# Gate products on the two 64-row halves of the array, and a tile of its own for the backward scan

## The chip, the cores and the metric

The kernel runs on one core of one Trainium2 chip. The metric is the device time of one execution in microseconds; the median of three runs before the change is 1204.66 (1204.58 to 1204.77). The engines are called by the profile's names: PE is TensorE (matmuls), PEld its weight loads, ACT is ScalarE, DVE is VectorE, POOL is GpSimd, SP is SyncE, which issues most DMAs.

## What is computed

Two layers over 512 tokens of 1024 channels, in float32. Each layer projects the normalised input to queries, keys, values, a recurrent input and a gate branch, runs neighbourhood attention (8 heads) beside a two-way gated recurrence (512 channels), normalises both, projects them back, and then runs a gated MLP with a width-3 convolution. The part that the change touches is the recurrence:

```python
def rg_lru(x, w_gate, b_gate, lam, reverse):
    bsz, s, _ = x.shape
    xb = x.reshape(bsz, s, N_LRU_BLOCKS, LRU_BLOCK)
    g = jnp.einsum("bsnc,gncd->gbsnd", xb, w_gate).reshape(2, bsz, s, D_LRU)
    g = g.astype(jnp.float32) + b_gate.astype(jnp.float32)[:, None, None, :]
    r_gate = jax.nn.sigmoid(g[0])
    i_gate = jax.nn.sigmoid(g[1])
    log_a = -LRU_C * r_gate * jax.nn.softplus(-lam.astype(jnp.float32))
    a = jnp.exp(log_a)
    u = jnp.sqrt(-jnp.expm1(2.0 * log_a)) * (i_gate * x.astype(jnp.float32))
    return linear_scan(a, u, reverse).astype(x.dtype)
...
        xc = depthwise_conv(x_rec, conv_lru_w[l], conv_lru_b[l], LRU_PAD)
        rec_f = rg_lru(xc, lru_w[l, 0], lru_b[l, 0], lru_lam[l, 0], reverse=False)
        rec_b = rg_lru(xc, lru_w[l, 1], lru_b[l, 1], lru_lam[l, 1], reverse=True)
        rec = (rec_f + rec_b) * jax.nn.gelu(gate, approximate=True)
```

The gate weights are block-diagonal: each of the 8 blocks of 64 channels has a 64x64 matrix per direction (forward, backward) and gate (r, i).

## The kernel before

Activations lie with channels in the 128 partitions and the 512 tokens in the free dimension, so an activation tile is 128x512. Every float32 operand of a large product is split into a rounded part and a rest (`hi`, `lo`, or names ending in `h`, `l`), and `mm3` (L243 to L245) makes a product of three matmuls: hi x hi, lo x hi, hi x lo. Weights come in chunks of up to 128x1024 by DMA (`raw`), are rounded on ACT (L205, `hi`) and subtracted on DVE (L206, `lo`), three chunks ahead of use. In layer 1 the gate, query, key and other input weights are not split in place: they were split during the MLP of layer 0 (`split_later`, L222 and L223), written to memory (`kept`), and are loaded in two halves as they are needed.

The mixing part of a layer follows a list of steps, `MIX`, which sets the order in the program text; a scheduler then orders each engine's instructions by it, with some marked urgent. `V` steps are value products, `c` the convolution of a block of 128 recurrent channels (`xc`, split into `xcs`), `t` the gates of such a block, `q`, `k` and `g` the query, key and gate-branch products (`a` and `b` are their halves of 12 matmuls), `S` the scores of a head, `T` the transposes of its probabilities (`ptw`, `pte`), `P` its product with the values (`o`), `u` copies of value edges on POOL, `e` the end of the gate branch (gelu, product with `fb`), `o` the output projection. PSUM banks come from small pools: three (`ps_mm`) for q, k, g and gate products, two for scores, two for transposes, one for `o`. A product can therefore wait for the bank that an earlier product's reader has not yet read.

`lru_gates` handles one block t of 128 channels, that is two of the 64-channel blocks. For each direction d and gate g it makes one full 128x128 product from a weight block that has the two 64x64 matrices on its diagonal and zeros elsewhere: 4 products of 3 matmuls (`gp`). ACT takes a tanh of each (L564: `w` for r, `ti` for i), then for each direction an exponential (`a`, L567), a tanh (L568), a square (L570), and one square root over both directions (L576, tile `w2` of 128x1024, of which there is one). DVE multiplies (L571, L572, L578), scans forward into `fb` (L581) and backward into `w` (L584), and adds the two (L586).

ACT's functions lie in tables, and a change of table is an instruction of its own (ACT_TABLE_LOAD). At the end of the kernel the scaled output is written in pieces of 4, 3 and 1 blocks (L485, L486).

Of the kernel before, what the change touches and what calls it, by code (L numbers as in the profile page):

```python
# [108 lines left out]
def encoder(ctx: ExitStack, tc: tile.TileContext, x_d, w_d, cols_d, bias_d, out_d):  # L109
# [102 lines left out]
    def split_later():  # L212
# [4 lines left out]
        for h in range(width(i) // 512):  # L217
            raw = p_t.tile([P, 512], F32, tag="t", name=f"lraw{i}{h}")
            nc.gpsimd.dma_start(raw, w_d[i][:, 512 * h:512 * h + 512])
            hi = p_fb.tile([P, 512], F32R, tag="fb", name=f"lhi{i}{h}")  # L220
            lo = p_fb.tile([P, 512], F32R, tag="fb", name=f"llo{i}{h}")
# [286 lines left out]
    def layer(l, xn):  # L508
# [24 lines left out]
        def convolve(t):  # L533
# [13 lines left out]
        pair = {}  # L547
# [2 lines left out]
        def lru_gates(t, ds):  # L550
            if 0 in ds:
                pair["c"] = chunk("gate", l, (t, 0))
            if 0 in ds:
                pair["w"], pair["work"] = p_w2.tile([P, 2 * T], F32, tag="w2", name=f"w2{l}{t}"), []
            c, both, work = pair["c"], pair["w"], pair["work"]
            for d in ds:
                w = both[:, d * T:(d + 1) * T]
                ti = big(p_t, "t", f"ti{l}{t}{d}")
# [6 lines left out]
                i = (l * 2 + d) * 4 + t  # L565
                a = big(p_t, "t", f"a{l}{t}{d}")
                nc.scalar.activation(a, w, AF.Exp, scale=spn[:, i:i + 1], bias=spn[:, i:i + 1])  # L567
# [421 lines left out]
```

## Time and profile before

| | |
|---|---|
| median of three runs | 1204.66 us (1204.58 to 1204.77) |
| the profiled execution, its span | 1204.35 us, 1202.6 us |
| mean granted clock | 0.996 |
| busy: PE, PEld | 1188.4 us (99%), 992.1 us (83%) |
| busy: DVE, ACT, POOL | 752.9 us (63%), 511.7 us (43%), 114.0 us (9%) |
| chain that ended last | PE 91%, ACT 4%, DVE 3% |
| where the gates lie | about 45 to 165 us (layer 0), 640 to 760 us (layer 1) |

The profiled execution is 1.75 us longer than its span. "Busy" is the sum of instruction durations; matmul records overlap, so the step from one start to the next tells what a matmul costs. Only a wait on PE, or more work on it, moves the end of this kernel directly; the idle time of the other engines matters where PE comes to need their result.

### The profile page before, as it was taken

Reading aid. Unit: us, or ns where it says so; the run is one execution under the profiler, and the core shown is the slowest. Engines: PE = TensorE matmul, PEld = TensorE weight load, DVE = VectorE, ACT = ScalarE, POOL = GpSimd, SP = SyncE. Lnnn points to the kernel's source line nnn. Section 1 sums busy time; section 2 is a strip of 40 time slices with the busy share of each in tenths; the row PEclk is TensorE's granted clock in tenths of the full one; section 3 lists DMA queues with packets and bytes.
Section 4 is the critical chain, followed back from the end, with each engine's and each line's share of the span. In section 5 each row is a group of like instructions: output and inputs, shape, how many; then the busy total and the mean of one; then the engine's idle time right before and its main releaser. Section 6 shows DMA issues by size and latency. Waiting matters only on the chain.

```text
span 1202.6 us, 14575 instructions
## 1 busy us (share of the span) xinstructions
PE 1188.4 (99%) x5534; PEld 992.1 (83%) x5534; DVE 752.9 (63%) x1226; ACT 511.7 (43%) x753; POOL 114.0 (9%) x230
## 2 busy tenths in 40 slices
PE   9999999999999999999999999999999999999996
PEld 8878888888888888888888888888888888888886
DVE  7988967776644567653736679587555336565443
ACT  6668854434321334422408578354233213333231
POOL 1102110123210122200002012000000000000000
PEclk9999999999999999999999999999999999999998
DMA  7222214376643376733256442232323232323222
GB/s 237 82 87 89 82 38 139 106 237 236 221 164 103 134 231 215 237 115 104 88 176 200 130 159 71 62 112 90 98 96 104 90 105 88 104 89 105 88 70 70
DMA packets 51046, 151.86 MB, mean 126 GB/s; under 512 B 6432, under 2 KB 9632, under 8 KB 50976
## 3 DMA queue, kind: packets, MB, share of 16 engines
q1 hardware_dynamic: 41792, 122.21, 31.1%
q0 software_dynamic: 8640, 28.32, 7.2%
q8 instruction: 43, 0.70, 0.2%
q10 hardware_dynamic: 544, 0.40, 0.1%
q14 instruction: 27, 0.22, 0.1%
HBM read 129.93 MB, written 20.97 MB: 125 GB/s over the span
## 4 chain that ended last, share of the span: by engine, by line
PE 91%; ACT 4%; DVE 3%; issue 1%; DVEq 0%; POOLq 0%; POOL 0%; ACTq 0%
PE dn L243 7%; PE dn L245 7%; PE dn L244 7%; PE pl L243 7%; PE pa L243 7%; PE pa L244 7%; PE pl L244 7%; PE pa L245 7%; PE pl L245 7%; PE out L245 2%; PE out L243 2%; PE out L244 2%; PE s L690 1%; PE xr L243 1%; PE up L243 1%; PE xr L244 1%
## 5 line engine op out<-in xcount | busy, mean ns | idle before, releaser
L205 ACT ACTIVATE hi<-raw 128x1024 fp32r<-128x1024 f32 (+1 forms) x189 | 197.6, 1046 | 380.5 <-PE dn L244 154.3
L206 DVE TENSOR_TENSOR lo<-raw,hi 128x1024 fp32r<-128x1024 f32 (+1 forms) x189 | 227.8, 1206 | 134.7 <-ACT hi L205 133.3
L845 DVE TENSOR_TENSOR ua<-pa,g_ffn_rb 128x512 f32<-128x512 f32 x44 | 30.4, 692 | 104.5 <-PE pa L245 104.5
L853 ACT ACTIVATE uc<-uc,cols 128x512 f32<-128x512 f32 x48 | 34.8, 724 | 116.2 <-DVE uc L851 116.1
L854 DVE TENSOR_TENSOR ua<-pl,uc 128x512 f32<-128x512 f32 x44 | 30.3, 689 | 45.0 <-PE pl L245 43.4
L467 POOL TENSOR_TENSOR fin_r<-fin_ms,expo 128x2 f32<-128x2 f32 x2 | 1.4, 696 | 377.0 <-DVE fin_ms L465 377.0
L851 DVE SCALAR_TENSOR_TENSOR uc<-ua,cols,uc 128x511 f32<-128x511 f32 x48 | 36.0, 751 | 1.6
L228 POOL DMA_DIRECT2D kept<-lhi x36 | 19.5, 542 | 182.1 <-ACT lhi L222 180.2
L849 DVE SCALAR_TENSOR_TENSOR uc<-ua,cols,uc 128x511 f32<-128x511 f32 x48 | 35.8, 746 | 0.1
L705 ACT ACTIVATE prob<-prob,mx 128x192 f32<-128x192 f32 (+1 forms) x64 | 27.5, 431 | 16.1 <-DVE mx L703 16.0
L223 DVE TENSOR_TENSOR llo<-lraw,lhi 128x512 fp32r<-128x512 f32 x36 | 24.7, 688 | 13.9 <-ACT lhi L222 13.9
L818 DVE TENSOR_TENSOR dns<-dn,g_ffn_rb 128x512 f32<-128x512 f32 x24 | 16.3, 689 | 24.8 <-PE dn L245 24.8
L222 ACT ACTIVATE lhi<-lraw 128x512 fp32r<-128x512 f32 x36 | 22.1, 616 | 8.0 <-DMA lraw<-in_w 8.0
L245 PE MATMUL out<-atth,lo 128*128 128x512 f32 x64 | 25.4, 397 | 0.0
L244 PE MATMUL out<-attl,hi 128*128 128x512 f32 x64 | 25.1, 394 | 0.0
L243 PE MATMUL out<-atth,hi 128*128 128x512 f32 x64 | 24.9, 402 | 0.0
L848 DVE TENSOR_SCALAR uc<-ua,cols 128x512 f32<-128x512 f32 x48 | 23.4, 488 | 1.5
L228 POOL DMA_DIRECT2D kept<-llo x36 | 19.5, 542 | 45.9 <-DVE llo L223 42.8
L690 PE MATMUL s<-k,q_pair 128*128 128x192 f32 (+1 forms) x128 | 22.7, 317 | 0.1
L640 POOL CAST edge<-vh 64x128 fp32r<-64x128 f32 x24 | 9.5, 394 | 120.3 <-ACT vh L627 55.9
L698 DVE CUSTOM_DVE_ANT_0 prob<-s,bias 128x192 f32<-128x192 f32 (+1 forms) x64 | 18.3, 337 | 3.9 <-PE s L690 3.6
L690 PEld LDWEIGHTS s<-k,q_pair 128*128 128x128 f32 x128 | 19.8, 190 | 1.0 <-DVE k L604 0.8
(935 smaller groups left out, 3633.6 us busy)
## 6 DMA issues: line engine op xcount, KB each, us to landing
raw<-in_w SPq DMA_DIRECT2D x183, 512.0 KB, 3.5
lraw<-in_w POOLq DMA_DIRECT2D x36, 256.0 KB, 4.6
kept<-lhi POOLq DMA_DIRECT2D x36, 256.0 KB, 2.5
kept<-llo POOLq DMA_DIRECT2D x36, 256.0 KB, 3.0
hi<-kept SPq DMA_DIRECT2D x36, 256.0 KB, 2.9
lo<-kept SPq DMA_DIRECT2D x36, 256.0 KB, 4.0
x<-in_x SPq DMA_DIRECT2D x8, 256.0 KB, 4.9
bias<-in_bias SPq DMA_DIRECT2D x8, 224.0 KB, 2.5
```

Of the source, the lines that this page charges most:

```text
L205: nc.scalar.activation(hi[:, sl], raw[:, sl], AF.Copy)
L206: nc.vector.tensor_tensor(out=lo[:, sl], in0=raw[:, sl], in1=f32(hi[:, sl]), op=ALU.subtract)
L228: nc.gpsimd.dma_start(d, f32(parts[h][n]))
L243: nc.tensor.matmul(ps, a[0], b[0], start=start, stop=False)
L244: nc.tensor.matmul(ps, a[0], b[1], start=False, stop=False)
L245: nc.tensor.matmul(ps, a[1], b[0], start=False, stop=stop)
L690: nc.tensor.matmul(ps[:, o:o + ROWS * w], q_pair[:, b], kt[:, ROWS * kc0:ROWS * (kc0 + w)], start=True, stop=True)
L845: nc.vector.tensor_tensor(out=by_row(ua), in0=natural(pa), in1=natural(rbf[0]), op=ALU.mult)
L849: nc.vector.scalar_tensor_tensor(out=c[:, 1:], in0=ua[:, :T - 1], scalar=w[0], in1=c[:, 1:], op0=ALU.mult, op1=ALU.add)
L851: nc.vector.scalar_tensor_tensor(out=c[:, :T - 1], in0=ua[:, 1:], scalar=w[2], in1=c[:, :T - 1], op0=ALU.mult, op1=ALU.add)
L853: nc.scalar.activation(c, c, AF.Gelu_apprx_tanh, bias=col("conv_ffn_b", j, l))
L854: nc.vector.tensor_tensor(out=natural(ua), in0=natural(pl_), in1=by_row(c), op=ALU.mult)
```

## The change

The weight block of a gate now holds, for each 64-channel block in its own 64 rows, the forward matrix in one half of the columns and the backward matrix in the other, with no zeros. For one gate g the product of rows 0 to 63 gives both directions of the first 64-channel block, that of rows 64 to 127 both directions of the second, in a bank each. For the second block the directions stand the other way round (n ^ d), so that the backward direction of the whole 128 channels lies in swapped halves: channel block 1 in rows 0 to 63. Each t step needs 2 weight blocks instead of 4, and the t steps are now divided by gate (`a` is gate r, `b` gate i) rather than by direction. Each bank is read by two tanhs of 64 rows. A swapped copy of `xc`, `xsw`, is made by two DMAs of GpSimd's queue. The backward scan writes a new tile, `back`, and two further DMAs, swapped again, add it into `fb`; the add on DVE is gone. `w2` is last read by the products with `ti`.

Beside that, `MIX` is changed: the first query product is in one piece, `k0` stands before `t1b`, the `t` and `e` steps of the later blocks stand later, the last `e` steps together. Chunks may be 256 wide. The last output is written in four pieces of two blocks.

```diff
-MIX = ("V0 c0 V1 V2 c1 V3 t0a V4 c2 V5 t0b V6 c3 V7 v q0a t1a q0b t1b k0 u0 "
+MIX = ("V0 c0 V1 V2 c1 V3 t0a V4 c2 V5 t0b V6 c3 V7 v q0 t1a k0 t1b u0 "
        "S0 k1a k1b g0a S1 q1a T0 q1b g0b P0 "
-       "S2 t2a k2a T1 k2b e0 t2b g1a P1 u1 S3 q2a T2 q2b g1b P2 "
-       "S4 t3a k3a T3 k3b e1 t3b g2a P3 u2 S5 q3a T4 q3b g2b P4 "
-       "S6 g3a T5 e2 g3b P5 u3 S7 o0 T6 o1 e3 o2 P6 T7 o3 o4 P7 o5 n o6").split()
+       "S2 k2a T1 t2a k2b g1a P1 u1 t2b S3 q2a T2 q2b g1b P2 "
+       "S4 e0 e1 k3a T3 t3a k3b g2a P3 u2 t3b S5 q3a T4 q3b g2b P4 "
+       "S6 g3a T5 g3b P5 u3 e2 e3 S7 o0 T6 o1 o2 P6 T7 o3 o4 P7 o5 n o6").split()
...
+            xc_sw[t] = big(p_h, "h", f"xsw{l}_{t}")
+            swapped(xc_sw[t], c)
...
+        rows_of = (slice(0, 64), slice(64, P))
+
+        def swapped(dst, src, **kw):
+            for n in range(2):
+                nc.gpsimd.dma_start(dst[rows_of[n]], src[rows_of[1 - n]], **kw)
...
-                for g, o in ((0, w), (1, ti)):
-                    ps = psum(ps_o if d and g and not o_ps[0] else ps_mm, f"gp{l}{t}{d}{g}")
-                    mm3(ps, blk(c, 2 * d + g), xcs[t], True, True)
-                    i = ((l * 2 + d) * 2 + g) * 4 + t
-                    with urgent():
-                        nc.scalar.activation(o, ps, AF.Tanh, scale=0.5, bias=half_b[:, i:i + 1])
...
+            def products(g, out):
+                ps = [psum(ps_o if n and g and not o_ps[0] else ps_mm, f"gp{l}{t}{g}{n}") for n in range(2)]
+                w = blk(gate["c"], g)
+                for a, b in ((0, 0), (0, 1), (1, 0)):
+                    for n, rows in enumerate(rows_of):
+                        nc.tensor.matmul(ps[n], w[a][rows], xcs[t][b][rows], start=a + b == 0, stop=a == 1)
+                for n in range(2):
+                    for d in range(2):
+                        i = ((l * 2 + d) * 2 + g) * 4 + t
+                        rows = rows_of[n ^ d]
+                        with urgent():
+                            nc.scalar.activation(out[d][rows], ps[n][rows], AF.Tanh, scale=0.5, bias=half_b[rows, i:i + 1])
...
-                    nc.vector.tensor_tensor_scan(out=w[:, ::-1], data0=a[:, ::-1], data1=ti[:, ::-1], initial=0.0,
-                                                 op0=ALU.mult, op1=ALU.add)
-                    nc.vector.tensor_tensor(out=fb[t], in0=fb[t], in1=w, op=ALU.add)
+                        back = big(p_t, "t", f"back{l}{t}")
+                        nc.vector.tensor_tensor_scan(out=back[:, ::-1], data0=a[:, ::-1], data1=u[:, ::-1], initial=0.0,
+                                                     op0=ALU.mult, op1=ALU.add)
+                        swapped(fb[t], back, accum_op=ALU.add)
...
-            for k, n in ((0, 4), (4, 3), (7, 1)):
-                o = probs_of[k // 4][:, k % 4:k % 4 + n]
...
+            for k in range(0, ND, 2):
+                o = probs_of[k // 4][:, k % 4:k % 4 + 2]
```

Three places show the new order. The first is PE at the gates of the second block of layer 0. In `gp` the digits are layer, block, then direction and gate before the change, and gate and row half after it. Before, from the first matmul of the second gate pair on:

```order
L243 MATMUL gp0110_709<-xcs0_1h_490,hi10_531 128x512
L244 MATMUL gp0110_709<-xcs0_1l_491,hi10_531 128x512
L245 MATMUL gp0110_709<-xcs0_1h_490,lo10_532 128x512
L243 MATMUL gp0111_714<-xcs0_1h_490,hi10_531 128x512
L244 MATMUL gp0111_714<-xcs0_1l_491,hi10_531 128x512
L245 MATMUL gp0111_714<-xcs0_1h_490,lo10_532 128x512
L243 MATMUL kps00_733<-xg_g_mix0_0h_179,hi11_595 128x512
L244 MATMUL kps00_733<-xg_g_mix0_0l_180,hi11_595 128x512
```

The same place after, where the query product `qps00` now runs whole ahead of all gates:

```order
L249 MATMUL qps00_668<-xg_g_mix0_7h_331,lo9_513 128x512
L577 MATMUL gp0100_708<-xcs0_1h_493,hi10_543 128x512
L577 MATMUL gp0101_709<-xcs0_1h_493,hi10_543 128x512
L577 MATMUL gp0100_708<-xcs0_1l_494,hi10_543 128x512
L577 MATMUL gp0101_709<-xcs0_1l_494,hi10_543 128x512
L577 MATMUL gp0100_708<-xcs0_1h_493,lo10_544 128x512
L577 MATMUL gp0101_709<-xcs0_1h_493,lo10_544 128x512
L577 MATMUL gp0111_768<-xcs0_1h_493,hi10_543 128x512
L577 MATMUL gp0111_768<-xcs0_1l_494,hi10_543 128x512
L577 MATMUL gp0111_768<-xcs0_1h_493,lo10_544 128x512
L247 MATMUL kps00_732<-xg_g_mix0_0h_179,hi11_610 128x512
...
L577 MATMUL gp0110_767<-xcs0_1h_493,hi10_543 128x512
```

The halves of gate r alternate; those of gate i are apart, `gp0111` ahead of the 24 matmuls of `kps00` and `gp0110` behind them.

The second place is DVE up to the reading of the first query product (`q_pair`), whose bank `kps00` takes. Before:

```order
L578 TENSOR_TENSOR ti000_513<-ti000_513,w200_512 128x512
L628 SCALAR_TENSOR_TENSOR vl02_643<-v0_2_426,g_mix0_r_345,vh02_642 128x512
L581 SCALAR_TENSOR_TENSOR fb00_590<-a000_524,ti000_513 128x512
L578 TENSOR_TENSOR ti001_570<-ti001_570,w200_512 128x512
L628 SCALAR_TENSOR_TENSOR vl03_647<-v0_3_427,g_mix0_r_345,vh03_646 128x512
L584 SCALAR_TENSOR_TENSOR w200_512<-a001_581,ti001_570 128x512
L206 TENSOR_TENSOR lo12_652<-raw12_599,hi12_651 128x1024
L596 TENSOR_TENSOR q_pair_169<-qps00_650,g_mix0_rb_370 64x8x64 x2
L586 TENSOR_TENSOR fb00_590<-fb00_590,w200_512 128x512
```

After:

```order
L602 TENSOR_TENSOR ti000_585<-ti000_585,w200_518 128x512
L602 TENSOR_TENSOR ti001_586<-ti001_586,w200_518 128x512
L605 SCALAR_TENSOR_TENSOR fb00_602<-a000_531,ti000_585 128x512
L609 SCALAR_TENSOR_TENSOR back00_606<-a001_532,ti001_586 128x512
L209 TENSOR_TENSOR lo11_611<-raw11_547,hi11_610 128x1024
L372 TENSOR_TENSOR xcs0_3l_634<-xc0_3_628,xcs0_3h_633 128x512
L209 TENSOR_TENSOR lo12_670<-raw12_614,hi12_669 128x1024
L653 SCALAR_TENSOR_TENSOR vl00_653<-v0_0_424,g_mix0_r_345,vh00_652 128x512
...
L653 SCALAR_TENSOR_TENSOR vl03_665<-v0_3_427,g_mix0_r_345,vh03_664 128x512
L621 TENSOR_TENSOR q_pair_169<-qps00_668,g_mix0_rb_370 64x8x64 x2
```

Between the square root's first reader and `q_pair` stand a second split of 1024, the split of `xcs0_3` and all four `vl` instead of two; the add into `fb` is gone.

The third place is the last block of layer 0, on PE and ACT. PE before, up to the query product `qps03` (`s054`, `s056` are scores of head 5, `prob1` its probabilities):

```order
L690 MATMUL s054_1422<-k02_1053,q_pair_169 128x192 x2
L690 MATMUL s056_1427<-k02_1053,q_pair_169 128x192
L690 MATMUL s056_1427<-k02_1053,q_pair_169 128x128
L243 MATMUL qps03_1442<-xg_g_mix0_0h_179,hi22_1262 128x512
```

PE after, from the gate's last matmul to `qps03`:

```order
L577 MATMUL gp0311_1434<-xcs0_3h_633,lo20_1087 128x512
L715 MATMUL s056_1463<-k02_1083,q_pair_169 128x192
L715 MATMUL s056_1463<-k02_1083,q_pair_169 128x128
L747 MATMUL ptw04_1497<-ident_154,prob0_159 128x128 x4
L751 MATMUL pte04_1498<-ident_154,prob0_159 128x128 x3
...
L247 MATMUL qps03_1478<-xg_g_mix0_0h_179,hi22_1298 128x512
```

ACT after, at the same place:

```order
L730 ACTIVATE prob1_160,sm05_1457<-prob1_160,mx05_1456 128x128
L593 ACTIVATE a2031_1361<-a031_1353 128x512
L383 ACTIVATE att0_sq_1416<-att01_1261 128x512
L583 ACTIVATE ti030_1431<-gp0310_1433,half_b_174 64x512
L583 ACTIVATE ti030_1431<-gp0311_1434,half_b_174 64x512
L583 ACTIVATE ti031_1432<-gp0310_1433,half_b_174 64x512
L583 ACTIVATE ti031_1432<-gp0311_1434,half_b_174 64x512
L598 ACT_TABLE_LOAD
```

The rest of the gate and the 12 matmuls of `gate02` (left out by the dots) moved ahead of `qps03`, and the four tanhs of gate i stand behind the exponentials of head 5, which before came after the whole block and its square root.

## Rows read from the trace of the kernel before

**Rows 1.** The page, part 1: busy time, share of the span, instructions.

```profile
PE 1188.4 (99%) x5534; PEld 992.1 (83%) x5534; DVE 752.9 (63%) x1226; ACT 511.7 (43%) x753; POOL 114.0 (9%) x230
```

**Rows 2.** Waits of PE: line, waited for, us in total, times, longest.

```profile
PE kps L243 <- DVE q_pair L596: 1.5, 1, 1.5
```

**Rows 3.** Windows: us, PE, PEld, DVE, ACT, POOL busy (instructions), clock, DMA share, GB/s.

```profile
90.00:105.00 15.00, 15.00 (x80) 12.75 (x79) 10.61 (x27) 14.33 (x27) 2.85 (x6) 1.00 0.28 89
...
120.00:135.00 15.00, 15.00 (x81) 12.77 (x80) 12.93 (x36) 14.12 (x26) 2.43 (x6) 1.00 0.36 117
...
700.00:715.00 15.00, 15.00 (x81) 12.88 (x80) 10.91 (x31) 9.33 (x21) 1.68 (x6) 1.00 0.44 141
```

**Rows 4.** Timeline of PE, second block: start, duration, instruction, [idle before it].

```profile
60.08 0.39 PE L243 MATMUL gp<-xcs_1h,hi 128*128 128x512 f32 x1
...
61.21 0.39 PE L245 MATMUL gp<-xcs_1h,lo 128*128 128x512 f32 x1
63.10 0.47 PE L243 MATMUL kps<-xg_g_mix_0h,hi 128*128 128x512 f32 x1 [1.50 <-DVE q_pair L596]
```

**Rows 5.** Timeline of PE: short matmuls, and a product after transposes.

```profile
95.77 0.47 PE L243 MATMUL kps<-xg_g_mix_4h,hi 128*128 128x512 f32 x1
96.09 0.39 PE L244 MATMUL kps<-xg_g_mix_4l,hi 128*128 128x512 f32 x1
...
104.38 0.28 PE L244 MATMUL o<-pt,edge 128*128 128x128 f32 x1
104.49 0.28 PE L245 MATMUL o<-pt,edge 128*128 128x128 f32 x1
```

**Rows 6.** Timeline of DVE around the first `q_pair`.

```profile
58.62 0.74 DVE L628 SCALAR_TENSOR_TENSOR vl<-v,g_mix_r,vh 128x512 fp32r<-128x512 f32 x1
59.28 1.21 DVE L584 TENSOR_TENSOR_SCAN w<-a,ti 128x512 f32<-128x512 f32 x1
60.41 1.24 DVE L206 TENSOR_TENSOR lo<-raw,hi 128x1024 fp32r<-128x1024 f32 x1
61.57 1.38 DVE L596 TENSOR_TENSOR q_pair<-qps,g_mix_rb 64x512 f32<-64x512 f32 x2
62.98 0.69 DVE L586 TENSOR_TENSOR fb<-fb,w 128x512 f32<-128x512 f32 x1
63.59 1.22 DVE L206 TENSOR_TENSOR lo<-raw,hi 128x1024 fp32r<-128x1024 f32 x1
```

**Rows 7.** Timeline of ACT: first square root, then tanhs, a square, a table load.

```profile
54.49 1.06 ACT L576 ACTIVATE w<-w 128x1024 f32<-128x1024 f32 x1
...
126.21 0.68 ACT L564 ACTIVATE w<-gp,half_b 128x512 f32<-128x512 f32 x1
126.78 0.63 ACT L379 ACTIVATE rec_sq<-fb 128x512 f32<-128x512 f32 x1
127.31 0.68 ACT L564 ACTIVATE ti<-gp,half_b 128x512 f32<-128x512 f32 x1
...
132.97 1.28 ACT L576 ACT_TABLE_LOAD   x1
```

**Rows 8.** Timelines of PE, DVE and ACT around the last block of layer 0.

```profile
130.48 1.41 PE L690 MATMUL s<-k,q_pair 128*128 128x192 f32 x8
131.65 0.48 PE L243 MATMUL qps<-xg_g_mix_0h,hi 128*128 128x512 f32 x1
...
131.70 0.36 DVE L698 CUSTOM_DVE_ANT_0 prob<-s,bias 128x192 f32<-128x192 f32 x1
...
136.63 0.46 ACT L705 ACTIVATE prob<-prob,mx 128x192 f32<-128x192 f32 x1
...
138.35 0.58 ACT L731 ACTIVATE pt<-ptw 128x512 fp32r<-128x512 f32 x1
```

**Rows 9.** The page, part 6: DMA issues, KB each, median us to landing.

```profile
kept<-llo POOLq DMA_DIRECT2D x36, 256.0 KB, 3.0
```

**Rows 10.** Timeline of all engines at the end: the last scaling.

```profile
1193.66 2.42 DVE L485 TENSOR_TENSOR prob<-prob,fin_rps 128x1024 f32<-128x1024 f32 x3 [1.55 <-PE fin_rps L474]
```

More of the change, by code (lines that the diff above doesn't have):

```diff
@@ L72, in weight_plan @@
             elif step[0] == "t" and step[-1] != "b":
-                plan.append(("gate", l, [(int(step[1]), dg) for dg in range(4)]))
+                plan.append(("gate", l, [(int(step[1]), g) for g in range(2)]))
             elif step[0] in IN_TILE and step[-1] != "b":
@@ L163, in width, with segments @@
         return P * len(plan[i][2])
+    def segments(i):
+        return [slice(a, min(a + 512, width(i))) for a in range(0, width(i), 512)]
     def is_kept(i):
@@ L178, in load_to @@
                 for n, t in enumerate((highs[i], lows[i])):
-                    for h in range(width(i) // 512):
-                        nc.sync.dma_start(f32(t[:, 512 * h:512 * h + 512]), kept[i][n, h])
+                    for h, sl in enumerate(segments(i)):
+                        nc.sync.dma_start(f32(t[:, sl]), kept[i][n, h])
                 state["load"] += 1
@@ L216, in split_later @@
         parts = []
[L217 to L221, printed above, removed]
+        for h, sl in enumerate(segments(i)):
+            n = sl.stop - sl.start
+            raw = p_t.tile([P, n], F32, tag="t", name=f"lraw{i}{h}")
+            nc.gpsimd.dma_start(raw, w_d[i][:, sl])
+            hi = p_fb.tile([P, n], F32R, tag="fb", name=f"lhi{i}{h}")
+            lo = p_fb.tile([P, n], F32R, tag="fb", name=f"llo{i}{h}")
             nc.scalar.activation(hi, raw, AF.Copy)
@@ L225, in split_later @@
         for n in range(2):
-            for h in range(width(i) // 512):
-                d = p_kept.tile([P, 512], F32, tag=f"kept{i}{n}{h}", name=f"kept{i}{n}{h}")
+            for h, sl in enumerate(segments(i)):
+                d = p_kept.tile([P, sl.stop - sl.start], F32, tag=f"kept{i}{n}{h}", name=f"kept{i}{n}{h}")
                 nc.gpsimd.dma_start(d, f32(parts[h][n]))
@@ L542, in convolve @@
             xcs[t] = plain_split(p_h, "h", c, f"xcs{l}_{t}")
+            xc_sw[t] = big(p_h, "h", f"xsw{l}_{t}")
+            swapped(xc_sw[t], c)
         fb = [None] * 4
[L547 removed]
+        gate = {}
         o_ps, att_t = [None], [None]
[L550 to L558, printed above, removed]
[L559 to L586 removed]
@@ L931, in lay_out @@
         blocks[n] = w.reshape(L, w.shape[1] // P, P, w.shape[2] // P, P).transpose(0, 1, 3, 2, 4)
-    gate = np.zeros((L, 4, 4, P, P), np.float32)
+    gate = np.empty((L, 4, 2, P, P), np.float32)
     for s in range(2):
         for d in range(2):
-            for g in range(2):
-                gate[:, :, 2 * d + g, 64 * s:64 * s + 64, 64 * s:64 * s + 64] = a["lru_w"][:, d, g, s::2]
+            o = 64 * (s ^ d)
+            gate[:, :, :, 64 * s:64 * s + 64, o:o + 64] = a["lru_w"][:, d, :, s::2].transpose(0, 2, 1, 3, 4)
     blocks["gate"] = gate
@@ L953, in lay_out @@
             put(COLS[n, l], a[n][l])
-    for n in ("lru_b", "lru_lam", "g_final"):
-        put(COLS[n], a[n])
+    lru = {}
+    for n in ("lru_b", "lru_lam"):
+        v = a[n].reshape(L, 2, -1, 2, 64).copy()
+        v[:, 1] = v[:, 1, :, ::-1]
+        lru[n] = v
+    for n, v in (("lru_b", lru["lru_b"]), ("lru_lam", lru["lru_lam"]), ("g_final", a["g_final"])):
+        put(COLS[n], v)
     rel = a["rel_bias"]
```

51 lines of the change are left out of this document (32 added, 19 removed).

## The prediction

> **What bounds the kernel now.** I read the shares by engine first, then what TensorE waited for, then the stretches in which the gates lie. TensorE (PE) is busy 99% of the span [rows 1]. Its waits, six groups of them in the whole trace, come to under 5 us; the largest, 1.5, is one `kps` product that waits for the vector engine to read a query product out [rows 2]. So TensorE's time is the kernel's time, and a matmul saved is time saved, as long as the other engines keep up. That condition is what I doubt. In the stretches with gates ScalarE and VectorE have little left: ScalarE 14.33 of 15 us from 90 to 105 and 14.12 from 120 to 135, VectorE 12.93 in the latter; in layer 1, where weight splits are kept from earlier, ScalarE is at 9.33 in 700:715 [rows 3].
>
> **The saving on TensorE.** The gate matmuls start 0.226 us apart (1.13 for five starts, [rows 4]). There are 12 for each of 4 blocks in 2 layers: 96, or 21.7 us. Afterwards there are 96 again, each on 64 rows of the array, meant to run two at a time: 48 x 0.226 = **10.8 us** at most. No row shows a 64-row matmul. If halves don't overlap, nothing is saved. If they do, a pair brings two weight loads; matmuls with little to stream start 0.11 apart (104.38 to 104.49, [rows 5]), so two loads fit into a pair's 0.226. I take the overlap as real, since the pair's operands and results touch no common row or bank. In the order as built seven pairs don't stand together: the three of `gp0110` and `gp0111` in each layer, with a whole `kps` product between them, and one of `gp0310` in layer 0. That leaves 41 x 0.226 = 9.3. Each change of the kind of work may cost: the nearest row is the product after transposes, whose second matmul starts 0.32 after the first where 0.23 is usual (95.77 to 96.09, [rows 5]). So 0.09 for each of two changes around some 18 groups: 3.2 us off. Bounds of the term: 0 to -10.8; taken -6.1, half in each layer.
>
> Of such changes the Trainium skill says more (TensorEngine Tiling (Array Packing), Tiling Modes): different tiles run in parallel, but changing the mode drains TensorE. No run here shows such a drain yet; [rows 5] show only the 0.09 between kinds of full-array work. Its page TensorE: Matmul & The Clock Gate, Part 3, gives 3.07 times for four tiles of 32 rows; an estimate from that share of the ideal (0.77) for two tiles makes 21.7 / 1.54 = 14.1, a saving of 7.6 in place of 10.8. Neither figure is used in the sum.
>
> **ScalarE.** The halves of one gate's two directions lie in different rows, so each of the 32 gate tanhs (16 a layer) becomes two over 64 rows: +16 a layer. Rows by 64 cost what 128 cost: two `q_pair` halves of 64x512 take 1.38 together, as long as two of 128x512 [rows 6]. A tanh takes 0.57 (126.21 to 126.78), a square 0.53, a table load 1.28 [rows 7]. Layer 0: 16 x 0.57 = 9.1, less two table loads 2.6, less smaller gate splits 0.6: **+5.9 us**. Layer 1: 9.1 less one load: +7.8. The first falls where ScalarE is at 95%, the second where it isn't.
>
> **VectorE.** The add of the backward scan into `fb` (0.69, or 0.61 up to the next start, [rows 6]) goes, 8 times. It becomes 16 DMAs from `back`, issued by GpSimd, which add into `fb`; 16 more bring the swapped `xsw`. No row shows an adding DMA; the nearest, `kept<-llo` on the same queue, lands in 3.0 us [rows 9]. Its users, the gelu products, come over 20 us later in the order, so I take nothing. Cover gone, up to 3 us a block would show. On GpSimd the edge copies for `o` stand behind issues that wait for a scan; the scan of that block is done long before those copies are due. `w2` is free for the next block after the products with `ti` rather than after scans and add, which lets ScalarE start earlier but moves no wait of TensorE.
>
> **Where it lands: layer 0, the second block.** With the earlier gates shorter and six matmuls moved, TensorE reaches `kps00` at about 59.4 instead of 61.4. It needs a bank that `q_pair` reads out. VectorE's new order puts ahead of that two products, two scans, two splits of 1024, one of 512 and four `vl`. I lay the square root's end at 53.6 (before, its record ended at 55.55, [rows 7]; two value copies of 0.6 and part of a weight split no longer stand ahead). Then 2 x 0.6 + 2 x 1.13 + 2 x 1.16 + 0.6 + 4 x 0.66 + 2 x 0.7 [rows 6] = 10.4: `q_pair` is done at 64.0, and `kps00` starts at 64.1, against 63.10 [rows 4]: +1.0. Three unpaired gate matmuls then still have to run, 0.7. **+1.7**, and the whole gain of the first two blocks, 2 us and more, is inside the longer wait (4.6 where 1.5 was).
>
> **The third and fourth block.** 12 pairs less one broken save 11 x 0.226 = 2.5; eight changes cost 0.7: -1.8. Two waits appear. First `o02`: the product `pt` that it needs now stands on VectorE behind `q_pair`, two products, both scans and two score tiles: 1.2 + 1.2 + 2.3 + 0.5 + 0.6 = 5.8 from the end of the query product. TensorE has 12 gate matmuls, the scores (1.17, [rows 8]) and five `kps` for that time, 5.1: +0.8. Second, and largest, `qps03`. It takes the bank that the third of four `ti` tanhs frees. On ScalarE these tanhs stand behind four exponentials that need the scores `s056`, and `s056` stands on TensorE behind the gate's last matmul. From the end of that gate: scores 0.7, two score tiles with their bias (0.3 each), a product and the maximum on VectorE 1.2, exponentials 1.72 (136.63 to 138.35, [rows 8]), a square and `att_sq` 1.06, three tanhs 1.71, handovers 0.2: 6.6 us. TensorE has scores, transposes and 12 gate matmuls to do: 4.0. **+2.6**; ScalarE has no slack here, so to 3.4: I take 3.0. Before, `qps03` came right behind the scores with no wait (130.48, 131.65, [rows 8]). Two smaller waits of the same kind (`o04` on its `pt`, `s060` on `q_pair`) I put at 0.7 together. Layer 0: 1.7 - 1.8 + 0.8 + 3.0 + 0.7 = **+4.4**.
>
> **Layer 1.** No splits of these weights there: `kps10` starts 0.7 earlier but has the three unpaired matmuls to come, 0. Blocks three and four: -1.8, with a wait of 0.4 at `qps13`: **-1.4**.
>
> **The end.** The last scaling goes out in four equal pieces instead of 4/3/1; the same 2.42 us of VectorE [rows 10], smaller last steps: -0.2 (0 to -0.5).
>
> **Sum.** 4.4 - 1.4 - 0.2 = +2.8 on the profiled 1204.35, which lies 0.3 below the median 1204.66; on the median's scale **1207.5 us**.
>
> **The rivals.** (a) *Faster*: ScalarE's and VectorE's chains are not as late as I lay them, because I summed a static order from single rows. The point from which it decides is `qps03`: if ScalarE is 2.6 us earlier there (exponentials ahead of their turn, faster half-row tanhs), that wait vanishes, and likewise at `kps00` if the square root ends 2 us earlier than I lay it. Then layer 0 comes to about -2.5, and with layer 1 at -3 to -4: 1197 to 1201, about 1199. For it: in the kernel before, ScalarE is as full in these stretches and TensorE waits hardly at all [rows 2, 3]. Against it: the 5.9 us more, on top of 14.33 and 14.12 of 15 [rows 3]. (b) *Within 0.2%*: the same terms with half the waits: 1203 to 1207. (c) *The halves don't run at once*, or changing to them costs far more than 0.09: TensorE gains nothing, and only the waits that ScalarE would have imposed anyway shrink. Then layer 1 loses its 1.8 and pays 1 to 2 for changes, layer 0 ends at +6: 1212 to 1214. That is also the case in which the change doesn't do what it says. What speaks for it is only that no row shows it working. By the rule of the Trainium skill (TensorEngine Tiling (Array Packing), Tiling Modes) a drain at each change would lead here.
>
> **How the numbers follow.** My forecast (1207 to 1210) has a chance of 0.38; (b) 0.28, (a) 0.24, (c) 0.10. A measurement of this kernel tells 0.2%, 2.4 us, from no change. Faster 0.24, same 0.28, slower 0.48. The range leaves out half of (a) and half of (c), under 2 in 10: 1198.5 to 1212.5. The likeliest side's own range, slower, is 1207 to 1213.
>
> **What would show it.** A wait `kps <- q_pair` of 4 to 5 us near 64, and one of about 3 us of `qps` on a `ti` tanh near 137 in layer 0 and hardly any in layer 1. Gate matmuls in pairs, the second starting almost with the first, a group of six taking about 0.7 plus 0.2 around it. ScalarE's busy time up by some 13 us, VectorE's down by about 6. It is wrong if the gate groups take 1.36 as before (c), or if TensorE's waits stay below 6 us in all (a), or if waits on adding DMAs appear, which I price at nothing.

## The result, and the profile after

The changed kernel takes 1217.36 us (1215.40 to 1219.27), the kernel before 1204.62: a ratio of 1.0106 with an interval of 1.0094 to 1.0118. It is 12.7 us slower, where I had put +2.8, and outside the range. Its runs lie in two groups, near 1215.5 (mean granted clock 0.994) and near 1219.2 (0.990). The profiled one is of the first: 1215.4 us, span 1213.6, which is 11.0 above the span before.

The page, part 1, of the kernel after (busy time, share, instructions), which answers [rows 1]:

```profile
PE 1190.5 (98%) x5534; PEld 984.5 (81%) x5534; DVE 746.9 (62%) x1219; ACT 529.0 (44%) x782; POOL 130.5 (11%) x262
```

ScalarE has 17.3 us more, VectorE 6.0 less. What TensorE waits for (line, releaser, us in total, times, longest) answers [rows 2]:

```profile
PE qps L247 <- ACT ti L583: 4.6, 4, 3.0
PE kps L247 <- DVE q_pair L621: 3.8, 1, 3.8
PE kps L247 <- issue: 2.5, 1, 2.5
PE o L248 <- DVE pt L757: 2.4, 3, 1.0
```

The third line is `kps10` in layer 1, put down to "issue"; it starts at 664.00, and `q_pair` ends at 663.90 (below), so it is the same wait as the second line. The windows of [rows 3], and two around the waits (columns as there; the eighth number is the granted clock):

```profile
60.00:75.00 15.00, 11.52 (x41) 8.98 (x42) 7.86 (x19) 10.98 (x17) 3.13 (x12) 0.77 0.40 118
...
120.00:135.00 15.00, 14.16 (x76) 11.03 (x76) 13.15 (x32) 11.71 (x23) 4.77 (x8) 1.00 0.33 90
135.00:150.00 15.00, 12.00 (x53) 9.57 (x53) 10.91 (x23) 12.98 (x24) 1.70 (x6) 0.89 0.26 85
...
700.00:715.00 15.00, 14.52 (x77) 11.82 (x76) 8.89 (x21) 14.77 (x27) 2.15 (x6) 1.00 0.54 173
```

The last line is not to be set against the 9.33 of [rows 3]: the kernel is some 10 us later there, and about the same work lay before the change in

```profile
690.00:705.00 15.00, 15.00 (x79) 12.67 (x78) 12.94 (x31) 12.75 (x23) 1.69 (x6) 1.00 0.47 138
```

So ScalarE goes from 12.75 of 15 us to 14.77 in that place. TensorE's timeline (start, us, instruction, idle before it) shows first a group of pairs, then the second block, [rows 4], the last block, [rows 8], and the second block of layer 1:

```profile
39.12 0.39 PE L249 MATMUL v<-hi,xg_g_mix_3l 128*128 128x512 f32 x1
39.44 0.50 PE L577 MATMUL gp<-xcs_0h,hi 64*128 64x512 f32 x2
39.77 0.40 PE L577 MATMUL gp<-xcs_0l,hi 64*128 64x512 f32 x2
40.01 0.40 PE L577 MATMUL gp<-xcs_0h,lo 64*128 64x512 f32 x2
40.33 0.50 PE L247 MATMUL v<-hi,xg_g_mix_4h 128*128 128x512 f32 x1
40.67 0.40 PE L248 MATMUL v<-lo,xg_g_mix_4h 128*128 128x512 f32 x1
...
59.26 0.39 PE L577 MATMUL gp<-xcs_1h,lo 64*128 64x512 f32 x1
63.48 0.77 PE L247 MATMUL kps<-xg_g_mix_0h,hi 128*128 128x512 f32 x1 [3.84 <-DVE q_pair L621]
64.05 0.63 PE L248 MATMUL kps<-xg_g_mix_0l,hi 128*128 128x512 f32 x1
...
68.32 0.63 PE L249 MATMUL kps<-xg_g_mix_3h,lo 128*128 128x512 f32 x1
68.74 0.43 PE L247 MATMUL kps<-xg_g_mix_4h,hi 128*128 128x512 f32 x1
69.01 0.39 PE L248 MATMUL kps<-xg_g_mix_4l,hi 128*128 128x512 f32 x1
...
143.60 0.56 PE L247 MATMUL qps<-xg_g_mix_0h,hi 128*128 128x512 f32 x1 [3.00 <-ACT ti L583]
143.96 0.63 PE L248 MATMUL qps<-xg_g_mix_0l,hi 128*128 128x512 f32 x1
144.39 0.63 PE L249 MATMUL qps<-xg_g_mix_0h,lo 128*128 128x512 f32 x1
...
664.00 0.47 PE L247 MATMUL kps<-xg_g_mix_0h,hi 128*128 128x512 f32 x1 [2.51 <-issue]
```

The pairs work: each "x2" is two matmuls in the time of one, and six take 0.89 us from the first start to the next product's (39.44 to 40.33) where six took 1.36. But after the wait of 3.84 us the next eleven steps, from 64.05 to 68.74, are 0.426 us apart instead of 0.228. That is the lower clock level, 1.2 GHz, and the window's granted clock of 0.77 says the same. It costs 2.4 us on top of the wait. From 143.96 to 146.95 it is again so. The granted clock had fallen at 62.0, 2.3 us into the first wait; the second time it fell at 143.9, 0.3 us after TensorE had begun again.

ScalarE and VectorE ahead of those waits (they answer [rows 7] and [rows 6]), and `q_pair` in layer 1:

```profile
47.65 2.65 ACT L583 ACTIVATE ti<-gp,half_b 64x512 f32<-64x512 f32 x4
...
51.92 1.06 ACT L598 ACTIVATE w<-w 128x1024 f32<-128x1024 f32 x1
```

```profile
53.01 1.29 DVE L602 TENSOR_TENSOR ti<-ti,w 128x512 f32<-128x512 f32 x2 [1.65 <-ACT w L598]
54.22 1.22 DVE L605 TENSOR_TENSOR_SCAN fb<-a,ti 128x512 f32<-128x512 f32 x1
...
56.47 1.20 DVE L209 TENSOR_TENSOR lo<-raw,hi 128x1024 fp32r<-128x1024 f32 x1
...
58.19 1.22 DVE L209 TENSOR_TENSOR lo<-raw,hi 128x1024 fp32r<-128x1024 f32 x1
...
61.96 1.38 DVE L621 TENSOR_TENSOR q_pair<-qps,g_mix_rb 64x512 f32<-64x512 f32 x2
...
662.53 1.37 DVE L621 TENSOR_TENSOR q_pair<-qps,g_mix_rb 64x512 f32<-64x512 f32 x2
```

The adding DMAs land in 3.2 us, like those of [rows 9]. The last scaling, [rows 10], still takes 2.48 us, but the kernel ends 6.7 us after the start of `fin_rps` instead of 9.7: 3.0 us back, a term that my sum lacked.

By layers, each counted from its own start, in the profiled execution:

| us against before | predicted | measured |
|---|---|---|
| layer 0 | +4.4 | +9.6 (TensorE's waits 8.4 instead of 1.85; its own time +3.1) |
| layer 1 | -1.4 | +4.4 (waits 5.0 instead of 0.25; own time -0.4) |
| end | -0.2 | -3.0 |
| sum | +2.8 | +11.0 |

### The profile page after: what moved, and what is told of

It reads as the page before. It is cut to its first block, busy times and chain, and to the rows that moved or that the text cites. A ratio compares the mean times of both kernels' runs of the same rounds, so it can differ in the third digit from the quotient of the medians.

```text
span 1213.6 us, 14690 instructions
## 1 busy us (share of the span) xinstructions
PE 1190.5 (98%) x5534; PEld 984.5 (81%) x5534; DVE 746.9 (62%) x1219; ACT 529.0 (44%) x782; POOL 130.5 (11%) x262
## 4 chain that ended last, share of the span: by engine, by line
PE 92%; ACT 3%; DVE 2%; issue 1%; DMA 1%; POOLq 0%; POOL 0%; DVEq 0%; SPq 0%; ACTq 0%
PE dn L249 7%; PE dn L248 7%; PE dn L247 7%; PE pl L249 7%; PE pa L249 7%; PE pa L247 7%; PE pl L247 7%; PE pl L248 7%; PE pa L248 7%; PE out L249 2%; PE out L247 2%; PE out L248 2%; PE kps L247 1%; PE s L715 1%; PE xr L247 1%
## 5 line engine op out<-in xcount | busy, mean ns | idle before, releaser
L208 ACT ACTIVATE hi<-raw 128x1024 fp32r<-128x1024 f32 (+2 forms) x189 | 196.6, 1041 | 380.6 <-PE dn L248 154.3
L209 DVE TENSOR_TENSOR lo<-raw,hi 128x1024 fp32r<-128x1024 f32 (+2 forms) x189 | 226.7, 1200 | 132.8 <-ACT hi L208 132.3
L227 DVE TENSOR_TENSOR llo<-lraw,lhi 128x512 fp32r<-128x512 f32 (+1 forms) x36 | 23.6, 658 | 12.0 <-ACT lhi L226 12.0
L226 ACT ACTIVATE lhi<-lraw 128x512 fp32r<-128x512 f32 (+1 forms) x36 | 21.3, 594 | 6.3 <-DMA lraw<-in_w 6.3
L560 POOL DMA_DIRECT2D fb<-back x16 | 13.4, 981 | 97.0 <-DVE back L609 81.0
L583 ACT ACTIVATE ti<-gp,half_b 64x512 f32<-64x512 f32 x32 | 21.1, 679 | 5.3 <-PE gp L577 4.9
```

The source lines that it names most:

```text
L208: nc.scalar.activation(hi[:, sl], raw[:, sl], AF.Copy)
L209: nc.vector.tensor_tensor(out=lo[:, sl], in0=raw[:, sl], in1=f32(hi[:, sl]), op=ALU.subtract)
```

## The experiments

**Order or halves.** The change moves steps and splits products. Theory A: the new order makes the long waits. Theory B: ScalarE's longer work does. Two kernels each take one part.

```diff
 e1_halves_old_order: the kernel after with the list MIX of before
 e2_full_gates_new_order: the kernel before with the list MIX of after
```

> The changed kernel with the step list of the kernel before: halves, doubled tanhs, own backward tile, adding DMAs and four-piece output stay, only the order goes back. Theory A (the new order puts q_pair and the ti tanhs late, and TensorE's clock falls to half after each wait of 3 us or more): the waits of 3.8 and 3.0 us go, the clock stays at 1.00 in all stretches of the gates, gates save about 6.5 us and the tail 3: 1194 to 1199 us. Theory B (16 more tanhs a layer on ScalarE make these waits in any order): waits of 3 us or more stay and the time is 1207 to 1215.

> The kernel before with the step list of the changed kernel: gates by 128 rows, one tanh each, add on VectorE, old output pieces; only the order is new. Theory A: the order alone makes the wait of kps on q_pair (3 to 4 us, and half the clock after it), 1207 to 1213 us. Theory B: without the doubled tanhs the order costs little: within 2 us of 1204.6.

The first took 1216.81 us (ratio 1.0102, 1.0087 to 1.0117), the second 1205.78 (1.0009, 1.0000 to 1.0019). The order alone costs 1.2 us; the halves cost the rest in either order, so theory A falls. Theory B's details were missed too: in the old order the time lies above its range, and the waits are spread (`qps` 3.3, `gp` on `q_pair` 2.1, `o` 2.8), none as long as 3 us. The clock still falls in three places there.

**The tanhs alone, and the halves without them.**

```diff
 e9_split_tanhs_alone (from before)
-                        nc.scalar.activation(o, ps, AF.Tanh, ...)
+                        for rows in (slice(0, 64), slice(64, P)):
+                            nc.scalar.activation(o[rows], ps[rows], AF.Tanh, ...)
 e5_one_tanh (from after)
-                for n in range(2):
-                    for d in range(2):
+                for d in range(2):
...
-                            nc.scalar.activation(out[d][rows], ps[n][rows], ...)
+                        nc.scalar.activation(out[d], ps[d], ...)
```

> The kernel before with each gate tanh split into two of 64 rows, nothing else: ScalarE's addition alone, without halves on TensorE, DMAs or a new order. Theory B: it alone makes the waits, TensorE waits 8 us or more in all and the time is 1210 to 1217. Theory A (the order): the time stays within 3 us of 1204.6.

> The changed kernel, but each bank of gate products is read by one tanh over all 128 rows, into the tile of one direction, instead of two of 64 rows that sort the halves: part of the channels of the two directions is exchanged and the output is another one, work and order otherwise as in the change. ScalarE has 16 tanhs (9.1 us) a layer less. Theory B (the doubled tanhs are the cause, in whatever order): the waits of qps on ti go, TensorE waits for 3 to 6 us in all, the gates keep their gain of about 6.5 us: 1196 to 1201 us. Theory C (the halves cost on TensorE, or the DMAs do): the waits stay and the time is 1211 or more.

Splitting the tanhs of the kernel before, with its full gates, gave 1218.39 us (1.0113, 1.0098 to 1.0128): the whole loss, and more than theory B's range. Merging them in the kernel after gave 1203.73 (0.9992, 0.9983 to 1.0001): all of the loss back, but not the gain of the gates that theory B's 1196 to 1201 counted on, and waits of `qps` on `ti` of 2.9 us stay. ScalarE's groups (busy us, mean ns of one), first after, then `e5_one_tanh`:

```profile
L583 ACT ACTIVATE w<-gp,half_b 64x512 f32<-64x512 f32 x32 | 21.3, 680 | 1.1 <-PE gp L577 0.6
L583 ACT ACTIVATE ti<-gp,half_b 64x512 f32<-64x512 f32 x32 | 21.1, 679 | 5.3 <-PE gp L577 4.9
```

```profile
L581 ACT ACTIVATE w<-gp,half_b 128x512 f32<-128x512 f32 x16 | 10.1, 680 | 0.6 <-PE gp L577 0.6
L581 ACT ACTIVATE ti<-gp,half_b 128x512 f32<-128x512 f32 x16 | 10.0, 677 | 0.6 <-PE gp L577 0.5
```

A tanh of 64 rows takes 680 ns, one of 128 rows 677 to 680. The doubled tanhs are the cause; open was how.

**How much ScalarE's length counts.** `e10_square_off_scalare` takes 16 other instructions off ScalarE. `e11_mixed_directions` is a version that keeps the whole computation with one tanh per bank: the directions stay mixed in a tile, and VectorE scans by half rows.

```diff
 e10_square_off_scalare (from after)
-                    nc.scalar.activation(a2, a, AF.Square)
+                    nc.gpsimd.tensor_tensor(out=a2, in0=a, in1=a, op=ALU.mult)
 e11_mixed_directions (from after; tanhs as in e5_one_tanh)
+            for rows in rows_of:
+                nc.gpsimd.dma_start(xc_sw[t][rows], c[rows_of[1]])
+            nc.gpsimd.dma_start(c[rows_of[1]], c[rows_of[0]])
...
+                    f, r = rows_of[d], rows_of[1 - d]
+                    nc.vector.tensor_tensor_scan(out=fb[t][f], data0=a[f], data1=u[f], ...)
+                    nc.vector.tensor_tensor_scan(out=back[r, ::-1], data0=a[r, ::-1], data1=u[r, ::-1], ...)
...
```

> The kernel after with one edit: the 16 squares a*a of the gates run on GpSimd instead of ScalarE; ScalarE then has about 16 x 0.6 = 9.6 us less of the 17.3 us that it gained. Theory B (the length of ScalarE's queue costs the time): about half of the 12.7 us comes back, 1207 to 1212. Rival (only the first bank's four tanhs in a row, ahead of the exps, make the waits; the number of ScalarE's instructions behind them is no matter): 1215 to 1219 as the kernel after.

> The kernel after with one 128-row tanh per bank, and the whole computation kept: each tile of 128 rows holds one direction in its upper half and the other in its lower half, three copies on GpSimd's queue give the convolution's halves twice, and VectorE runs four scans of 64 rows per tile instead of two of 128 (16 more scans, about 1.1 us each by the scans of 128 rows, 18 us on VectorE). Theory B: ScalarE's 17 us were the cause, and VectorE, busy 62% of the span, has room: 1203 to 1207. Rival (any engine that this stretch waits for costs as much as ScalarE did): 1212 or more.

They took 1214.56 us (1.0087, 1.0073 to 1.0101) and 1219.59 (1.0122, 1.0107 to 1.0138). With ScalarE 7.4 us shorter than after (521.6), 2.8 us came back, less than theory B wanted and more than its rival. With ScalarE as short as before (508.3) and 16 more scans on VectorE, the whole loss stayed. So ScalarE's length as such is not the price. VectorE in `e5_one_tanh`, then in `e11_mixed_directions`:

```profile
53.30 1.23 DVE L603 TENSOR_TENSOR_SCAN fb<-a,ti 128x512 f32<-128x512 f32 x1
54.44 1.21 DVE L607 TENSOR_TENSOR_SCAN back<-a,ti 128x512 f32<-128x512 f32 x1
...
59.97 1.38 DVE L619 TENSOR_TENSOR q_pair<-qps,g_mix_rb 64x512 f32<-64x512 f32 x2
```

```profile
53.69 1.21 DVE L607 TENSOR_TENSOR_SCAN fb<-a,ti 64x512 f32<-64x512 f32 x1
54.91 1.22 DVE L609 TENSOR_TENSOR_SCAN back<-a,ti 64x512 f32<-64x512 f32 x1
56.05 1.20 DVE L607 TENSOR_TENSOR_SCAN fb<-a,ti 64x512 f32<-64x512 f32 x1
57.26 1.22 DVE L609 TENSOR_TENSOR_SCAN back<-a,ti 64x512 f32<-64x512 f32 x1
...
62.23 1.38 DVE L621 TENSOR_TENSOR q_pair<-qps,g_mix_rb 64x512 f32<-64x512 f32 x2
```

The two more scans put 2.3 us ahead of `q_pair`, and it starts 2.3 us later. (What else differs cancels: the square root ends 0.6 later, and one `vl` of 0.66 stands behind `q_pair` instead of ahead.) The place of the first `kps` across kernels:

| kernel | square root ends | `q_pair` ends | `kps00` waits | clock, 60 to 75 us |
|---|---|---|---|---|
| before | 55.55 | 62.95 | 1.50 | 1.00 |
| after | 52.98 | 63.34 | 3.84 | 0.77 |
| `e5_one_tanh` | 51.87 | 61.35 | 1.56 | 1.00 |
| `e10_square_off_scalare` | 53.67 | 62.30 | 2.05 | 1.00 |
| `e11_mixed_directions` | 52.44 | 63.61 | 4.07 | 0.77 |
| `e13_ti_whole` (below) | 51.86 | 62.23 | 2.45 | 0.89 |
| `e14_w_whole` (below) | 53.26 | 61.88 | 1.90 | 1.00 |

So this wait is made in the chain from the tanhs over square root and scans to `q_pair`, whichever engine an added instruction stands on. The next two runs call this theory C (the theory C of `e5_one_tanh` and `e6_no_swap_dmas` was another, and is out).

**Inside and outside that chain.** Two kernels merge half of the tanhs each; in both, half the rows of the merged tiles belong to the other direction.

```diff
 e13_ti_whole: the kernel after, with the tanhs of g == 1 merged as in e5_one_tanh
 e14_w_whole: the kernel after, with the tanhs of g == 0 merged so
```

> The kernel after with one 128-row tanh per bank for the second product of each tile (ti) only; half of its rows then belong to the other direction, so the output is another. ScalarE has 8 instructions a layer more than before instead of 16. Theory C (what counts is the place in the in-order chain ti tanhs, square root, scans, q_pair): this bank stands in that chain, so kps00 waits about 2.5 us instead of 3.8 and qps03 about 1.7 instead of 3.0, the clock between 60 and 75 us stays at full, and most of the 12.7 us comes back: 1205 to 1209. Rival (each tanh more costs the same wherever it stands): half comes back, 1210 to 1212.

> The counterpart: one 128-row tanh per bank for the first product (w) only, whose exponentials are not what the square root waits for last. Theory C: the waits at kps00 and qps03 stay within 0.7 us of 3.8 and 3.0, and the clock falls after them; 1211 to 1217. Rival (each tanh costs the same): 1210 to 1212, and both waits about 1 us shorter.

They took 1208.86 us (1.0032, 1.0020 to 1.0045) and 1209.08 (1.0037, 1.0024 to 1.0050). For `ti` theory C had the time and the wait at `kps00` right (2.45), but not the clock, which fell behind that wait (0.89), nor `qps03` (0.76 where it said 1.7). For `w` it was wrong: both waits are short (1.90 and 0.85), and the time lies below its range and its rival's. So theory C falls in its narrow form: the `w` tanhs are worth as much as the `ti` tanhs. The table shows one way how: in `e14_w_whole` the square root ends later than after, and yet `q_pair` sooner. VectorE in that kernel:

```profile
49.08 1.22 DVE L209 TENSOR_TENSOR lo<-raw,hi 128x1024 fp32r<-128x1024 f32 x1
...
57.39 1.21 DVE L209 TENSOR_TENSOR lo<-raw,hi 128x1024 fp32r<-128x1024 f32 x1
...
60.50 1.38 DVE L621 TENSOR_TENSOR q_pair<-qps,g_mix_rb 64x512 f32<-64x512 f32 x2
```

After, two weight splits of 1.2 us stand between the scans and `q_pair` (56.47 and 58.19 above), and VectorE is idle for 1.65 us ahead of the square root's result. Here one of them runs ahead of that result (49.08), as in `e5_one_tanh`, `e10` and `e11`. So what the tanhs cost depends also on the order that the scheduler builds around them. Nor do the parts add: either half gives back 8.3 to 8.5 us, both together 13.6. And a wait can move: in `e14_w_whole` the last block of layer 1 waits 3.9 us on a `ti` tanh, where after it waits 0.4. Shown is that the doubled tanhs cause the loss, and at `kps00` by which queues; how it divides among the other places stays open.

**The clock after a wait.**

```diff
 e4_filled_wait (from after)
+                if l == 0 and t == g == 1:
+                    for _ in range(8):
+                        nc.tensor.matmul(ps[1], w[0], xcs[t][0], start=True, stop=True)
```

> The changed kernel with 8 idle matmuls (1.8 us) put into the wait of kps00 in layer 0, into a bank that the real product overwrites; the work and its order are otherwise the same. If the wait makes the clock fall: what is left of the wait is about 2 us, as short as the one of 2.5 us in layer 1 that keeps the clock, the 12 matmuls at half speed go, and the time falls by 2.4 us, to 1213.0 against 1215.4 (or 1216.8 against 1219.2). If the clock falls for another reason: half speed stays and the time is the same as the changed kernel's.

It took 1215.41 us (1.0090, 1.0075 to 1.0105). The wait fell to 1.64, and the clock still dropped:

```profile
58.90 2.11 PE L577 MATMUL gp<-xcs_1h,hi 128*128 128x512 f32 x8
...
63.53 0.77 PE L247 MATMUL kps<-xg_g_mix_0h,hi 128*128 128x512 f32 x1 [1.64 <-DVE q_pair L624]
64.09 0.63 PE L248 MATMUL kps<-xg_g_mix_0l,hi 128*128 128x512 f32 x1
...
143.01 0.50 PE L247 MATMUL qps<-xg_g_mix_0h,hi 128*128 128x512 f32 x1 [3.00 <-ACT ti L586]
143.34 0.39 PE L248 MATMUL qps<-xg_g_mix_0l,hi 128*128 128x512 f32 x1
143.57 0.40 PE L249 MATMUL qps<-xg_g_mix_0h,lo 128*128 128x512 f32 x1
```

So filling most of a wait did not keep the clock at `kps00`, while at `qps03` the same wait of 3.00 us as after now passes without a drop. In layer 1 it is the other way round: `kps10` waits 2.51 us as after, and here the clock falls behind it. The same window in the kernel after, then here (the eighth number is the clock):

```profile
660.00:675.00 15.00, 12.49 (x58) 9.71 (x59) 8.33 (x19) 12.31 (x17) 4.58 (x6) 1.00 0.63 183
```

```profile
660.00:675.00 15.00, 12.49 (x49) 9.74 (x49) 7.07 (x18) 11.96 (x17) 3.33 (x5) 0.89 0.56 168
```

The length of a wait alone does not decide; what does stays open.

**The end.** Five kernels look for the 3.0 us after `fin_rps`.

```diff
 e3_tail_only: the kernel before, the output in four pieces of 2 as after
 e6_no_swap_dmas: the kernel after, without its 32 DMAs; xsw is xc
 e8_more_pe_instructions: the kernel before, 8 one-column matmuls at its start
 e12_before_with_idle_dmas (from before)
+            xsw[t] = big(p_h, "h", f"xsw{l}_{t}")
+            swapped(xsw[t], c)
...
+                    swapped(xsw[t], fb[t])
 e15_half_the_idle_dmas: the same without the last line
```

> The kernel before with the output in four pieces of two blocks instead of 4, 3 and 1; nothing else. If the 3.0 us between the last statistics product and the end of the span (9.7 us before, 6.7 after) come from the pieces, 1201.6 us (1201.2 to 1202.2). If they come from something else in the change, 1204.6. The prediction's own term for it was 0.2 to 0.5 us.

> The changed kernel without the 32 DMAs of half tiles: the second direction takes the unswapped input, and the backward scan isn't added into fb, so the output is another one. Theory B: nothing waits for these DMAs, the time is the changed kernel's within 2 us (1214 to 1219). Theory C, as far as it names the DMAs: at least 4 us less.

> The kernel before with 8 more matmuls of one column among the warming ones at the start (16 more instructions of TensorE). At the end of the kernel SyncE waits 2.2 to 3.0 us for TensorE's queue in before, e2 and e3, and 0.5 in the changed kernel, e1 and e4, which have 15 or more instructions more on TensorE. If the place of the last instructions in TensorE's stream decides: the wait falls to 0.5 and the time to 1202.4, plus at most 0.4 for the matmuls themselves. If it is the halves or something else: 1204.6 to 1205.0.

> The kernel before with 32 DMAs more on GpSimd's queue, as many and as large as those of the kernel after, into a tile that nobody reads. If the number of GpSimd's DMAs in the program sets how long the kernel's end takes after the last output (6.4 us before, 3.4 us after), the end is short and the time is 1201.5 to 1202.5. Rival (the end is short for another reason in the kernels with halves): 1204.6.

> The kernel before with 16 idle DMAs on GpSimd's queue instead of 32. If each of them shortens the end by the same amount, half of the 1.9 us that 32 gave: 1203.6. If what counts is a number that is passed or not, 1202.7 or 1204.6.

The times: 1204.41 us (0.9999), 1219.84 (1.0125), 1209.54 (1.0025), 1202.68 (0.9987, 0.9978 to 0.9996), 1202.25 (0.9982, 0.9973 to 0.9991). SyncE's waits on TensorE's queue at the program's last line (us, times, longest), in before and in `e12_before_with_idle_dmas`:

```profile
SPq L983 <- PEq L983: 2.7, 2, 2.2
```

```profile
SPq L992 <- PEq L992: 0.7, 2, 0.5
```

Four pieces gain nothing (the wait grows to 3.0), and TensorE's instruction count does not change it (2.2). That kernel is slower at its start: in the profiled run, 1209.86 us, the added matmuls take 3.3 us where I allowed 0.4, and the `xr` products behind them start 0.43 us apart until 13.6 us, where before they are 0.23 apart from 6.1 on; three of its seven runs took 1205.4 to 1205.8. Without the DMAs the long end returns (3.1), and the layers take no less than after (602.7 and 599.8 us, after 602.1 and 599.8), so leaving these DMAs out gains nothing in them. With 32 or 16 idle DMAs the kernel before gets the short wait. So it goes with GpSimd's DMAs, not with the halves, and not in proportion to their number. Why is open. It is not the whole of the 3.0 us: from the start of `fin_rps` to the end these two kernels take 7.4 us, before 9.6, after 6.7. The 0.7 left over may be the four pieces, which only a short wait would let show: `e3_tail_only` and `e6_no_swap_dmas`, with four pieces and the long wait, take 9.6. No run has that alone. These two kernels keep the whole computation and beat the kernel before, by 1.9 and 2.4 us, and so the kernel after.

## Why the prediction was wrong

**TensorE's saving: right in the gates, not beside them.** I took -6.1 for the pairs, half in each layer, changes of kind included. The `gp` matmuls take 3.0 us less in layer 0 and 3.5 in layer 1, and a pair runs in the time of one. But a change of kind costs about twice the 0.09 that I put, since it lengthens the step on either side of it: in the group shown, the steps from 39.12 to 39.44, on to 39.77, from 40.01 to 40.33 and on to 40.67 take 0.32 to 0.34 us, against 0.23 to 0.24. Two of these four belong to the neighbours. So this group brings 0.27 us in all, where I had 0.50. The Trainium skill (TensorEngine Tiling (Array Packing), Tiling Modes) has a drain at each such change; these rows put it at about 0.2 us here. In layer 1, where the clock stays full, TensorE's own time is only 0.4 us less than before: `v`, beside two groups, has 0.4 more, `o` 0.9, `gate` 0.8, and how much of the last two the changes make is open. So rival (c) is out in its first half, the halves do run at once; its second half, dearer changes, held in part, and its 1212 to 1214 is nearer than mine.

**The waits of layer 0: right where I named them.** `kps00` waits 3.84 (4.6 predicted; `q_pair` ends at 63.34, 64.0 predicted), `qps03` 3.00 (3.0), `o02` 0.84 (0.8). The 0.7 for two small ones was luck: neither `o04` nor `s060` waits, and a `qps` wait of 0.72 that I did not name stands in their place. The sum is 8.4 against 9.1.

**The step that failed in layer 0** is that TensorE runs at its old pace behind a wait, a term that I put at nothing without a reason. My +4.4 holds -2.9 of own time; measured is +3.1. Of these 5.9 us, 4.0 are the slow steps behind the two longest waits (2.4 in `kps`, 1.6 in `qps`), at the lower clock level as the rows above show; the rest lies in steps beside the gate groups and in places that I did not trace to a cause. No view of the gates before had a row for it: the longest wait was 1.5, the clock 1.00. The Trainium skill (TensorE: Matmul & The Clock Gate, Part 1) says that the low level is the default and activity lifts it. The stretches after 63.48 and 143.60 agree, in that the clock rose again under matmuls; the one after the 2.51 us at 664.00 does not show it.

**The step that failed in layer 1** is the "0" at `kps10`, and that `qps13` (0.4, measured 0.40) was to be the only wait. I read one window with ScalarE at 9.33 of 15 us [rows 3] as room for 7.8 us more. The window before it was fuller (12.75 from 690 to 705), and a mean does not see a queue: ahead of `kps10` ScalarE's gate tanhs come in two runs of 2.65 us in front of the square root, which ends 0.8 us later than before, counted from the layer's start. TensorE reached `kps10` 1.6 us sooner than before, `q_pair` ended only 0.6 sooner, and `kps10` started 0.6 later where I had 0.7 earlier. Part of that is the order: before, `kps10` started ahead of the end of `q_pair` (654.96) and waited for something else,

```profile
653.80 0.50 PE L243 MATMUL kps<-xg_g_mix_0h,hi 128*128 128x512 f32 x1 [0.25 <-ACT w L564]
```

while in the new order with full gates (`e2_full_gates_new_order`) it already waits 0.97 us, until `q_pair` ends. All waits of the layer come to 5.0 us against 0.4: 4.6 of the 5.8 that I missed. The rest is TensorE's own time.

**The end** was sized by the smaller last steps (-0.2). Of the 3.0 us, 2.2 go with 32 DMAs on another queue, which had no term.

**The sum.** 5.2 us too little in layer 0, 5.8 in layer 1, 2.8 too much at the end: 8.2 on the profiled execution. The median lies 2 us above that execution. My price of ScalarE (13.7 us more, measured 17.3) entered the sum only at the two waits that I had laid out by hand. `e9_split_tanhs_alone` shows that the same work costs 13.7 us with no halves at all, in sixteen waits of up to 2.0 us: 11.7 us in the two layers, 2.1 before.

**Where the gain went.** Even with the tanhs merged the halves bring little: `e5_one_tanh` is 1 us behind `e12_before_with_idle_dmas`, which has the same short wait at its end and full gates. Against the kernel before, its `gp` time is 7.6 us less, but its waits are 3.8 us more and TensorE's other products take 6.0 us more (1.3 of it in a `qps` where the clock fell). `v` has 0.44 us more in each layer in it and after, and none in `e2_full_gates_new_order`, so that part comes with the halves; the rest is not divided.

## What to carry to other kernels

When a change doubles instructions on an engine that stands between two products of the bounding engine, count them ahead of every product that waits for a bank, not only at the latest one; a low mean share is no slack where the queue is in order. Splitting a result by rows halves nothing for the engines that read it: a 64-row tanh cost what a 128-row one cost. When short products of another kind are put between full ones, price the steps of the neighbours too. Price a wait on TensorE with the slower matmuls that may follow it, as a range, since one and the same wait came with and without them.

## What was not expected of the hardware

After a wait of 3.84 us twelve matmuls ran 0.43 us apart; after one of 2.51 in the same kernel, or 2.05 in `e10_square_off_scalare`, none did. After 1.64 behind eight extra matmuls, 2.45 in `e13_ti_whole` and 2.51 in `e4_filled_wait` some did, and after 3.00 some did in one kernel and none in another. The kernel's last wait of SyncE on TensorE's queue is 2.2 to 3.1 us with 108 DMAs on GpSimd's queue and 0.5 with 124 to 148, in all sixteen kernels here.
